# Sums of weight blocks and of hidden values for seven block products, made on VectorE in place of GpSimd

## Chip, cores and metric

The kernel runs on one core of one Trainium2 chip. The metric is the device time of one execution in microseconds (us). The engines are named as in the profile: PE (TensorE matmuls), PEld (its weight loads), DVE (VectorE), ACT (ScalarE), POOL (GpSimd) and SP (SyncE, which here issues the DMAs). Each engine runs its instructions in the order in which they stand; between engines semaphores do the waiting.

## The reference, cut to what matters

A decoder trunk of 4 layers works on 256 tokens of width 1024, in float32. Every layer has a feed-forward network (FFN), a token mixer (window attention, gated linear attention, RWKV-7, window attention again) and a second FFN, so there are eight FFNs.

```python
def swiglu(x, w_in, w_out):
    gate, up = jnp.split(x @ w_in, 2, axis=-1)
    return (jax.nn.silu(gate) * up) @ w_out

for layer in range(DEPTH):                        # DEPTH = 4, D_FF = 2816
    ff = swiglu(rmsnorm(h, g[0]), ffn_w_in[layer, 0], ffn_w_out[layer, 0])
    h = h + 0.5 * rmsnorm(ff, g[1])
    ...                                           # the layer's mixer
    ff = swiglu(rmsnorm(h, g[4]), ffn_w_in[layer, 1], ffn_w_out[layer, 1])
    h = h + 0.5 * rmsnorm(ff, g[5])
```

## The kernel before

Matmuls run in a one-pass format that holds fewer bits than float32. So every operand is **split** into a high part, copied and rounded by ACT, and a low part, value minus high part, which DVE computes with a `tensor_tensor` subtract. Each product is then three matmuls (`mm3`): high by high, high by low, low by high. Every weight block that comes from memory therefore costs one DMA, one ACT instruction and one DVE instruction over 128x512 values before PE can use it (`weight`).

An FFN's 2816 middle columns are cut into 11 chunks of 256. Chunks 0 and 1 are computed tokens first (`tokens`): one PSUM bank per token tile and chunk, 24 matmuls of 512 columns. Chunks 2 to 10 are a loop with two halves of 128 middle columns each. In a half PE makes 48 matmuls of 256 columns (gate and up for both token tiles) into one PSUM bank `p`. Then DVE reads the gate out of it (`sg`, in the profile `hf<-ps,m` of 128x256), ACT copies the up part out (`hf<-ps`), ACT takes a tanh, and two DVE instructions make the hidden values (`hf<-hf,hf`, `m<-hf,hf`). Only after the copy is `p` free for the next half.

The second matrix product of a chunk is a 2x2 by 2x2 block product (tokens in two halves, middle columns in two halves, output columns in two halves). It is made from **seven** block products in place of eight, which needs sums of blocks on both sides. On the side of the weights `weights(c)` loads four 128x512 blocks of `w_out` and makes four differences T1 to T4 from them; T2 needs T1 and T4 needs T2. On the side of the hidden values `hidden(th)` makes four 128x128 sums s1 to s4 into one tile `S`; s2 needs s1 and s4 needs s2. All of them are then split by ACT and DVE, and `products` runs 3 matmuls of 512 columns for each of the seven. The seven results stay in seven PSUM banks `acc` over all chunks. There are eight banks, so in the loop one is left for `p`. In the loop, 12 of these matmuls stand after a chunk's first half and 9 after its second; in the last chunks 6 of the 9 are put off to the end of the FFN.

The order within each engine is not the order of the code. All calls are recorded, and `schedule` sets them by a plan with costs for every instruction and a latency between engines: on each engine, the call that can start first comes next. In that plan a `tensor_tensor` of n columns costs 120 + 1.1 n ns on POOL and 70 + 1.04 n ns on DVE. Splits of weights and the weight differences may be taken ahead of their time (`kind = "split"`). Buffers of 128x512 values (tag `m`, 87 of them) are given out by the same plan, and SP, which issues all loads in order, waits for a buffer to come free. All instructions are issued from one line of `emit`, L471; L469 issues the few matmuls that keep the clock up.

The names that matter: `GT` (line 760) is the engine call that makes T1 to T4 in `weights` (line 779) and s1 to s4 in `hidden` (line 796).

Of the kernel before, what the change touches and what calls it, by code (L numbers as in the profile page):

```python
# [480 lines left out]
class Trunk:  # L481
# [264 lines left out]
    def ffn(self, l, f, start):  # L746
# [8 lines left out]
        nc = self.nc  # L755
# [1 line left out]
        w_out = self.a["ffn_w_out"][l, f].rearrange("(k p) n -> p k n", p=P)  # L757
        n0 = 6 * l + 4 * f
        uh, ul = ([self.m2([P, 2, NT, P], F32R) for _ in range(4)] for _ in "hl")
        GT = nc.gpsimd.tensor_tensor  # L760

        def load_in(c, k):
            return self.once(("ffn", l, f, c, k), lambda: self.weight(
# [8 lines left out]
        def split(x, dt):  # L772

            hi, lo = dt(), dt()
            nc.scalar.activation(hi[:], x, AF.Copy)
            nc.vector.tensor_tensor(lo[:], x, hi[:], ALU.subtract)
            return hi, lo

        def weights(c):
# [9 lines left out]
            for n, x, y in ((1, b[1, 2], b[1, 1]), (2, b[2, 2], T[1]), (4, b[2, 1], T[2]), (3, b[2, 2], b[1, 2])):  # L789
                GT(T[n][:], x[:], y[:], ALU.subtract)  # L790
            r = {n: split(w[:], lambda: self.m2(dt=F32R)) for n, w in (
# [4 lines left out]
        def hidden(th):  # L796
# [3 lines left out]
            s = [None] + [S[:, n, :] for n in range(4)]  # L800
            GT(s[1], a21, a22, ALU.add)
            GT(s[2], s[1], a11, ALU.subtract)
            GT(s[3], a11, a21, ALU.subtract)
            GT(s[4], a12, s[2], ALU.subtract)
            three = th[:].rearrange("p j t n -> p (j t) n")[:, :3]
# [932 lines left out]
```

## Time and profile before

| | |
|---|---|
| median of 3 runs | 2399.59 us (2398.52 to 2401.42) |
| the profiled execution | 2397.45 us, span from first to last instruction 2395.5 us |
| busy over the span | PE 2109.6, DVE 2029.5, ACT 1368.8, POOL 899.8 us |
| instructions | PE 14120, DVE 3292, ACT 3000, POOL 889 |
| mean granted clock of TensorE | 0.958 of full speed |
| read from memory | 351.64 MB |

A row that groups instructions says which engine, operation and tiles (output, arrow, inputs), the shape (partitions x columns), how many, how long they were busy together, the mean duration of one in ns, and the engine's idle time just before them with what ended it. DVE starts an instruction before the one ahead has fully ended, so durations add up to more than busy time. The granted clock is 1.00 at 2.4 GHz and 0.50 at 1.2 GHz; a stretch between has parts of both.

### The profile page before, as it was taken

What the parts mean: (1) busy time and instruction counts of PE and PEld (TensorE: products, weight loads), DVE (VectorE), ACT (ScalarE), POOL (GpSimd) and SP (SyncE); (2) the same over time, 40 slices, a digit from 0 to 9 for tenths busy, and PEclk for the clock granted to TensorE, in tenths of its full rate; (3) what the DMA queues carried; (4) which work ended last, traced back from release to release, by engine and by line L of the source; (5) the groups of instructions that cost most, each with busy time, mean ns of one, the idle gap of its engine ahead of it and who ended that gap; (6) DMA issues with size and microseconds to landing.
All of it is one profiled execution on the core that took longest, in us unless ns stands there. A gap on an engine that the chain in (4) does not pass through costs nothing. (4 is left out here: it accounts for less than half of the span.)

```text
span 2395.5 us, 41720 instructions
## 1 busy us (share of the span) xinstructions
PE 2109.6 (88%) x14120; PEld 1818.6 (76%) x14120; DVE 2029.5 (85%) x3292; ACT 1368.8 (57%) x3000; POOL 899.8 (38%) x889
## 2 busy tenths in 40 slices
PE   7888998888888998988888889998888888898887
PEld 6787768786777776877678768887877678777776
DVE  8887989888987988888888798588888987888887
ACT  6554666555654865555554566565555655566553
POOL 4443035435543005442644222135442544205442
PEclk8999999999999999999999999999999999999998
DMA  7555345554564454555455421454555455444551
GB/s 229 155 163 178 123 148 157 159 154 139 163 175 148 123 171 136 161 162 160 134 171 151 140 89 54 126 171 128 162 160 160 136 167 170 139 148 148 161 161 57
DMA packets 444902, 355.47 MB, mean 148 GB/s; under 512 B 33372, under 2 KB 364304, under 8 KB 444688
## 3 DMA queue, kind: packets, MB, share of 16 engines
q1 hardware_dynamic: 444688, 352.82, 48.9%
q8 instruction: 110, 1.80, 0.3%
q14 instruction: 104, 0.85, 0.1%
HBM read 351.64 MB, written 1.05 MB: 147 GB/s over the span
## 5 line engine op out<-in xcount | busy, mean ns | idle before, releaser
L471 PE MATMUL ps<-m,m 128*128 128x256 f32 (+4 forms) x12248 | 1976.2, 326 | 217.4 <-ACT hf L471 139.1
L471 PEld LDWEIGHTS ps<-m,m 128*128 128x128 f32 (+2 forms) x12248 | 1665.7, 193 | 457.8 <-ACT hf L471 177.6
L471 DVE TENSOR_TENSOR m<-m,m 128x512 fp32r<-128x512 f32 (+1 forms) x1814 | 1385.1, 816 | 148.3 <-ACT m L471 144.8
L471 ACT ACTIVATE m<-m 128x512 fp32r<-128x512 f32 (+4 forms) x1838 | 1003.8, 610 | 437.0 <-POOL m L471 335.2
L471 POOL TENSOR_TENSOR m<-m,m 128x512 f32<-128x512 f32 (+1 forms) x528 | 656.9, 1258 | 351.3 <-DMA m<-in_ffn_w_out_dram 194.6
L471 POOL TENSOR_TENSOR m<-m 128x128 f32<-128x128 f32 x176 | 131.1, 764 | 534.2 <-DVE m L471 321.1
L471 ACT ACTIVATE hf<-ps 128x256 f32<-128x256 f32 (+1 forms) x166 | 62.3, 377 | 266.4 <-DVE hf L471 244.4
L471 POOL TENSOR_TENSOR ti<-ti,nhalf 128x1 f32<-128x1 f32 (+2 forms) x60 | 50.9, 849 | 379.6 <-DVE ti L471 371.3
L471 ACT ACTIVATE m<-ps 128x512 f32<-128x512 f32 (+4 forms) x219 | 109.5, 525 | 134.2 <-PE ps L471 132.6
L471 DVE SCALAR_TENSOR_TENSOR hf<-hf,hf 128x256 f32<-128x256 f32 x144 | 99.6, 692 | 60.1 <-ACT hf L471 60.0
L471 DVE TENSOR_TENSOR m<-hf,hf 128x256 f32<-128x256 f32 x144 | 115.5, 802 | 5.0
L471 POOL TENSOR_SCALAR_AFFINE_SELECT m<-m 128x512 f32<-128x512 f32 (+1 forms) x54 | 38.6, 733 | 182.7 <-ACT m L471 182.3
L471 DVE TENSOR_TENSOR m<-m,ps 128x512 f32<-128x512 f32 (+1 forms) x112 | 60.4, 568 | 25.3 <-PE ps L471 23.3
L471 ACT ACTIVATE hf<-hf 128x256 f32<-128x256 f32 x144 | 58.9, 409 | 40.0 <-DVE hf L471 40.0
L471 DVE TENSOR_TENSOR hf<-ps,m 128x256 f32<-128x256 f32 x144 | 59.7, 415 | 21.7 <-PE ps L471 17.2
L471 PE MATMUL ps<-ident,m 128*128 128x128 f32 (+1 forms) x344 | 58.8, 281 | 4.7 <-DVE m L471 3.7
L471 ACT ACTIVATE m<-ps,gT 128x128 fp32r<-128x128 f32 (+1 forms) x192 | 53.6, 377 | 15.4 <-PE ps L471 9.1
L471 PEld LDWEIGHTS ps<-ident,m 128*128 128x128 f32 (+1 forms) x344 | 41.4, 144 | 18.5 <-DVE m L471 6.4
L471 PE MATMUL ps<-ident,hf 128*128 128x128 f32 x68 | 15.2, 308 | 45.4 <-DVE hf L471 45.4
L471 DVE SCALAR_TENSOR_TENSOR m<-ps,gT,m 128x128 fp32r<-128x128 f32 x176 | 48.5, 341 | 3.8 <-ACT m L471 3.4
L471 PEld LDWEIGHTS ps<-ident,hf 128*128 128x128 f32 x68 | 7.9, 148 | 55.1 <-DVE hf L471 38.9
L471 ACT ACTIVATE junk<-h 128x512 bf16<-128x512 f32 x48 | 30.2, 629 | 29.2 <-DVE h L471 26.7
(101 smaller groups left out, 764.1 us busy)
## 6 DMA issues: line engine op xcount, KB each, us to landing
m<-in_ffn_w_in_dram SPq DMA_DIRECT2D x1152, 128.0 KB, 2.9
m<-in_ffn_w_out_dram SPq DMA_DIRECT2D x352, 256.0 KB, 3.6
m<-in_ffn_w_in_dram SPq DMA_DIRECT2D x128, 256.0 KB, 3.8
m<-in_swa_w_qkv_dram SPq DMA_DIRECT2D x48, 256.0 KB, 2.9
m<-in_rwkv_w_rkv_dram SPq DMA_DIRECT2D x48, 256.0 KB, 3.4
m<-in_gla_w_in_dram SPq DMA_DIRECT2D x40, 256.0 KB, 3.2
m<-in_swa_w_o_dram SPq DMA_DIRECT2D x32, 256.0 KB, 2.7
m<-in_norm_g_dram SPq DMA_DIRECT2D x24, 256.0 KB, 4.8
```

What stands on the lines that cost most here:

```text
L471: getattr(getattr(self.nc, o.eng), fn)(*[fix(v) for v in args], **{k: fix(v) for k, v in kw.items()})
```

## The change

`GT` becomes the same call of DVE. The 88 chunks have eight such calls each, 704 in all. The function computes what it computed before; nothing else in the code differs.

```diff
@@ -757,7 +757,7 @@
         uh, ul = ([self.m2([P, 2, NT, P], F32R) for _ in range(4)] for _ in "hl")
-        GT = nc.gpsimd.tensor_tensor
+        GT = nc.vector.tensor_tensor
```

Because the plan's costs and the engine are others, the scheduler sets a new order for the whole program. Here is DVE's row in the third FFN, in the loop, from one reading of `p` by DVE (`hf<-ps,m`) on. The names are numbered by tile, so the same role has another number in the two programs. Before, the row is the reading, splits, and the next reading:

```order
L471 TENSOR_TENSOR hf_140_8121<-ps_156_8024,m_1423_6828 128x256
L471 TENSOR_TENSOR m_1707_8125<-m_1664_7904,m_1679_7985 128x512
L471 SCALAR_TENSOR_TENSOR hf_142_8130<-hf_142_8130,hf_140_8121 128x256
L471 TENSOR_TENSOR m_1708_8137<-hf_141_8127,hf_142_8130 128x256
L471 TENSOR_TENSOR m_1718_8159<-m_1662_7900,m_1680_7992 128x512
L471 TENSOR_TENSOR m_1721_8170<-m_1677_7975,m_1681_7995 128x512
L471 TENSOR_TENSOR m_1722_8177<-m_1668_7916,m_1682_8001 128x512
L471 TENSOR_TENSOR m_1723_8184<-m_1674_7959,m_1683_8004 128x512
L471 TENSOR_TENSOR m_1724_8191<-m_1675_7963,m_1685_8019 128x512
L471 TENSOR_TENSOR m_1725_8198<-m_1676_7971,m_1686_8021 128x512
L471 TENSOR_TENSOR hf_143_8247<-ps_157_8168,m_1423_6828 128x256
```

Now T1 (`m_1747`, from blocks `m_1705` and `m_1704`) stands just ahead of the reading, T3 (`m_1750`) in the row after T2 (`m_1749`) right behind it, and T4 (`m_1760`) after the second product of the hidden values; splits follow:

```order
L471 TENSOR_TENSOR m_1747_8349<-m_1705_8140,m_1704_8138 128x512
L471 TENSOR_TENSOR hf_146_8355<-ps_158_8259,m_1459_7015 128x256
L471 TENSOR_TENSOR m_1749_8361<-m_1703_8136,m_1747_8349 128x512
L471 TENSOR_TENSOR m_1750_8369<-m_1703_8136,m_1705_8140 128x512
L471 SCALAR_TENSOR_TENSOR hf_148_8367<-hf_148_8367,hf_146_8355 128x256
L471 TENSOR_TENSOR m_1753_8381<-hf_147_8364,hf_148_8367 128x256
L471 TENSOR_TENSOR m_1760_8397<-m_1702_8134,m_1749_8361 128x512
L471 TENSOR_TENSOR m_1762_8407<-m_1704_8138,m_1707_8146 128x512
L471 TENSOR_TENSOR m_1765_8420<-m_1702_8134,m_1709_8155 128x512
L471 TENSOR_TENSOR m_1768_8432<-m_1703_8136,m_1715_8178 128x512
```

So three of the four differences stand between a reading of `p` and the next, and one ahead of it.

POOL's row at the same place before holds a chunk's four differences and four sums and nothing else:

```order
L471 TENSOR_TENSOR m_1713_8147<-m_1712_8145,m_1711_8143 128x512
L471 TENSOR_TENSOR m_1714_8149<-m_1710_8141,m_1712_8145 128x512
L471 TENSOR_TENSOR m_1716_8153<-m_1710_8141,m_1713_8147 128x512
L471 TENSOR_TENSOR m_1729_8224<-m_1709_8139,m_1716_8153 128x512
L471 TENSOR_TENSOR m_1741_8281<-m_1708_8137 128x128 x2
L471 TENSOR_TENSOR m_1741_8281<-m_1741_8281,m_1708_8137 128x128
L471 TENSOR_TENSOR m_1741_8281<-m_1708_8137,m_1741_8281 128x128
```

The sums stand now in DVE's row, in the chunk's second half, between the second product of the hidden values (`m_1701`) and the splits of the sums (`m_1734`):

```order
L471 TENSOR_TENSOR hf_144_8245<-ps_157_8150,m_1459_7015 128x256
L471 TENSOR_TENSOR m_1728_8248<-m_1661_7923,m_1671_7969 128x512
L471 SCALAR_TENSOR_TENSOR hf_145_8251<-hf_145_8251,hf_144_8245 128x256
L471 TENSOR_TENSOR m_1701_8132<-hf_143_8241,hf_145_8251 128x256
L471 TENSOR_TENSOR m_1729_8264<-m_1701_8132 128x128 x2
L471 TENSOR_TENSOR m_1729_8264<-m_1729_8264,m_1701_8132 128x128
L471 TENSOR_TENSOR m_1731_8275<-m_1701_8132,m_1730_8266 128x384
L471 TENSOR_TENSOR m_1729_8264<-m_1701_8132,m_1729_8264 128x128
L471 TENSOR_TENSOR m_1732_8283<-m_1667_7953,m_1673_7978 128x512
L471 TENSOR_TENSOR m_1734_8294<-m_1729_8264,m_1733_8287 128x512
```

POOL's row keeps no instruction of the FFNs but the inverse roots of the norms.

## Rows read from the trace of the kernel before

**Rows 1.** The page's first part: busy time, share, instructions of each engine.

```profile
PE 2109.6 (88%) x14120; PEld 1818.6 (76%) x14120; DVE 2029.5 (85%) x3292; ACT 1368.8 (57%) x3000; POOL 899.8 (38%) x889
```

**Rows 2.** Stretches: length, busy time by engine, granted clock, DMA share and rate; eight loops.

```profile
55.00:228.60 173.60, 151.14 (x1039) 139.43 (x1038) 147.49 (x204) 94.07 (x187) 71.25 (x65) 0.96 0.55 163
...
1175.60:1355.00 179.40, 154.93 (x1039) 143.36 (x1038) 150.40 (x208) 95.69 (x191) 76.64 (x80) 0.93 0.52 155
...
sum 1404.30, PE 1218.83 PEld 1122.94 DVE 1195.42 ACT 760.09 POOL 593.46; mean PE 152.35 PEld 140.37 DVE 149.43 ACT 95.01 POOL 74.18
```

**Rows 3.** The same view of a stretch ahead of a loop and of two between FFNs.

```profile
337.00:363.90 26.90, 20.76 (x82) 15.99 (x82) 25.13 (x33) 16.65 (x38) 23.27 (x19) 0.87 0.45 136
...
245.00:330.00 85.00, 84.71 (x487) 64.95 (x487) 75.35 (x182) 54.37 (x167) 5.49 (x8) 1.00 0.46 142
800.00:900.00 100.00, 99.17 (x655) 80.07 (x655) 91.44 (x185) 75.64 (x157) 4.97 (x6) 1.00 0.53 162
```

**Rows 4.** PE in order of time: start, length of a run, count, idle time before it.

```profile
645.25 8.03 PE L471 MATMUL ps<-m,m 128*128 128x256 f32 x57 [0.74 <-ACT hf L471]
654.87 8.71 PE L471 MATMUL ps<-m,m 128*128 128x256 f32 x60 [1.59 <-ACT hf L471]
```

**Rows 5.** DVE in order of time, one chunk of the third FFN's loop.

```profile
640.74 3.70 DVE L471 TENSOR_TENSOR m<-m,m 128x512 fp32r<-128x512 f32 x6 [1.55 <-ACT m L471]
...
645.54 1.28 DVE L471 SCALAR_TENSOR_TENSOR hf<-hf,hf 128x256 f32<-128x256 f32 x1 [0.16 <-ACT hf L471]
646.85 1.41 DVE L471 TENSOR_TENSOR m<-hf,hf 128x256 f32<-128x256 f32 x1
648.18 5.88 DVE L471 TENSOR_TENSOR m<-m,m 128x512 fp32r<-128x512 f32 x6
653.99 0.41 DVE L471 TENSOR_TENSOR hf<-ps,m 128x256 f32<-128x256 f32 x1
654.32 0.68 DVE L471 TENSOR_TENSOR m<-m,m 128x512 fp32r<-128x512 f32 x1
655.16 0.43 DVE L471 SCALAR_TENSOR_TENSOR hf<-hf,hf 128x256 f32<-128x256 f32 x1 [0.15 <-ACT hf L471]
655.62 0.42 DVE L471 TENSOR_TENSOR m<-hf,hf 128x256 f32<-128x256 f32 x1
655.96 2.29 DVE L471 TENSOR_TENSOR m<-m,m 128x512 fp32r<-128x512 f32 x3
```

**Rows 6.** POOL in order of time, the same chunk.

```profile
645.01 6.09 POOL L471 TENSOR_TENSOR m<-m,m 128x512 f32<-128x512 f32 x4 [4.97 <-DMA m<-in_ffn_w_out_dram]
656.17 1.52 POOL L471 TENSOR_TENSOR m<-m 128x128 f32<-128x128 f32 x2 [5.07 <-ACT m L471]
657.66 1.44 POOL L471 TENSOR_TENSOR m<-m,m 128x128 f32<-128x128 f32 x2
```

**Rows 7.** Groups of DVE, whole span: count, busy us, mean ns, idle before.

```profile
L471 DVE TENSOR_TENSOR m<-m,m 128x512 fp32r<-128x512 f32 x1620 | 1264.9, 834 | 137.5 <-ACT m L471 136.5
L471 DVE TENSOR_TENSOR m<-hf,hf 128x256 f32<-128x256 f32 x144 | 115.5, 802 | 5.0
L471 DVE SCALAR_TENSOR_TENSOR hf<-hf,hf 128x256 f32<-128x256 f32 x144 | 99.6, 692 | 60.1 <-ACT hf L471 60.0
```

**Rows 8.** The same view of DVE, 245 to 330 us alone.

```profile
L471 DVE TENSOR_TENSOR m<-m,m 128x512 fp32r<-128x512 f32 x48 | 30.2, 684 | 0.0
```

**Rows 9.** Groups of POOL, whole span.

```profile
L471 POOL TENSOR_TENSOR m<-m,m 128x512 f32<-128x512 f32 x352 | 539.4, 1553 | 344.6 <-DMA m<-in_ffn_w_out_dram 194.6 <-DVE m L471 50.7 <-ACT m L471 38.3
L471 POOL TENSOR_TENSOR m<-m 128x128 f32<-128x128 f32 x176 | 131.1, 764 | 534.2 <-DVE m L471 321.1 <-ACT m L471 181.1 <-PE ps L471 31.9
L471 POOL TENSOR_TENSOR m<-m,m 128x128 f32<-128x128 f32 x176 | 117.8, 669 | 6.7
```

**Rows 10.** Loads of `w_out`, 600 to 720 us: from issue to landing.

```profile
DMA to landing us min/median/max: 2.4/3.0/4.4
```

**Rows 11.** DVE in order of time, chunk 0 of the second FFN.

```profile
344.94 5.74 DVE L471 TENSOR_TENSOR m<-m,m 128x512 fp32r<-128x512 f32 x4
```

## The prediction, on record before the changed kernel ran

> **What bounds the kernel now.** I read the page's first two parts first: over the span PE is busy 2109.6 us and DVE 2029.5 us of 2395.5, POOL 899.8 [rows 1]. Two engines near 85% over a program of many stages say little, so I cut the span into stretches. The kernel has eight FFNs, and in each of them chunks 2 to 10 run as a loop of about 175 us; the eight loops together take 1404.3 us, of which PE is busy 1218.8, so PE stands still for 185.5 us in them by the sum in [rows 2]. A stretch between two FFNs looks different: in 800 to 900 us POOL is busy 5.0 of 100 us, DVE 91.4, and PE 99.2 at full granted clock; in 245 to 330 us it is 5.5, 75.4 and 84.7 of 85 [rows 3]. So PE is not stopped by a DVE that is busy 91%; it is stopped where POOL works.
>
> The loop shows how. PE alternates between a run of 8.03 us (48 matmuls of the hidden values, then 9 products) followed by a wait of 1.59, and a run of 8.71 us (48 and 12) followed by 0.74 [rows 4]. The waits end with ACT's copy out of the one PSUM bank that the seven accumulators leave free; that copy stands behind DVE's read of the same bank (`hf<-ps,m`, called the evacuation below), because DVE is in order and reads it first. A chunk is thus 16.74 us of PE work and about 2.33 us of waiting.
>
> Why is the evacuation late? In the run that begins at 645.25 PE has finished the 48 matmuls at about 651.2 (653.28 less 9 products; the run of 60 is 0.68 longer than that of 57, so 0.227 each). DVE reaches the evacuation at 653.99 [rows 5], since six splits before it took 5.88 us. Six of the same splits took 3.70 at 640.74 [rows 5]: 0.684 for one, and (3.70 - 0.684)/5 = 0.603 from one start to the next. The difference, 2.18 us, falls where POOL makes the chunk's four differences of weight blocks, 645.01 to 651.10 [rows 6]. The two DVE instructions just before are stretched as well, 1.28 and 1.41 us against 0.43 and 0.42 half a chunk later, where POOL rests [rows 5]. So each 128x512 operation of POOL stops DVE for about 1.0 us, (0.85 + 0.99 + 2.18)/4. Over the program the three largest DVE groups with two SBUF inputs have means of 834, 802 and 692 ns [rows 7], where the first takes 684 in the stretch without POOL work [rows 8] and the others 0.42 and 0.43: 1620 x 0.150 + 144 x 0.38 + 144 x 0.26 = 335 us of DVE time that is only waiting for POOL.
>
> The other half of the chunk loses in a chain: POOL's four 128x128 sums take 656.17 to 659.10, ACT splits them only then, and DVE idles 1.55 us for ACT (one row shown, of the chunk before) [rows 5, 6].
>
> **What the change removes.** All 704 operations of this kind leave POOL: 352 of 128x512 at 1553 ns and 352 of 128x128 at 764 and 669 ns [rows 9]. With them go the stretch on DVE, about 4.0 us per chunk from the weights and 0.5 from the sums (655.96: three instructions in 2.29 us, about 1.75 alone [rows 5]), and the idle 1.55 us. Nothing else hides behind POOL; what remains there are square roots and masks.
>
> **What it adds.** DVE gets the same 704. A 128x512 one goes at the 0.603 us pace, so 2.4 us per chunk for four. No 128x128 operation of this form runs on DVE before. Its pace is bounded by the 256-column evacuation (0.33 from 653.99... to the next start at 654.32 [rows 5]) and, by the slope (0.603 - 0.33)/256 per column, 0.19; two of the four need the result just made, so I take 0.25 each, 1.0 us per chunk. DVE's chunk before, without the stretch: 16 instructions of 512 columns x 0.603 = 9.65, one of 384 (0.47 by the same slope), and two evacuations with their two followers 2 x (0.33 + 0.46 + 0.34) = 2.26; together 12.4 us. After: 12.4 + 3.4 = **15.8 us per chunk, under PE's 16.74** (94%). Before, with 4.5 us of stretch and the idle times, DVE came to about 19, and that was the period: it was DVE's row that PE waited for.
>
> **What moves.** The scheduler orders anew by its costs. In DVE's row the first difference of a chunk now stands just ahead of an evacuation, the second to fourth right behind it, and the four sums behind the second product of the hidden values. In the order the four buffers for a chunk's `w_out` were last read by matmuls about a hundred rows, some 14 us of PE work, ahead of the first difference, and such a load lands 2.4 to 4.4 us after its issue [rows 10]; so DVE should not have to wait for it. I cost that at nothing; if it fails, every evacuation behind it waits too (the third rival). In the order 120 clock-keeping matmuls stand where 115 stood: nothing.
>
> **The sum**, against the profiled execution (span 2395.5, time 2397.45):
> 1. Idle PE in the eight loops is 185.5. The nearest rows without POOL work leave PE idle under 1% [rows 3], 1.5 us per loop; since DVE's margin is 6% and two late halves of each FFN carry more DVE rows than PE can cover, I leave 3 us per loop, 24. Gain 161. Ends: 13 us per loop left (81) and 1 left (177).
> 2. PE's busy time in the loops is itself longer than its work. Work is 9 x 16.74 less 18 products that the last three chunks put off (4.1), 146.6 per loop, 1172.8 in all, against 1218.8: 46 us, and the granted clock there is 0.93 to 0.96, 1.00 in the busy stretches [rows 2, 3]. PE at half clock follows its waits; I give back 60%, 27 us. Ends 0 and 46.
> 3. Chunks 0 and 1, eight stretches like 337 to 363.9: DVE is busy 25.13 of 26.9, PE 20.76 [rows 3]. Eight differences and eight sums move in: 8 x 0.603 + 8 x 0.25 = 6.8 us; out goes the stretch, 8 x 1.0 and a little. Four splits there take 5.74 instead of 2.49 [rows 11], 1.08 for each of three POOL operations, so about 8.8 goes. Net gain 2 us, 16 in all. Ends 0 and 5 each.
> Sum 161 + 27 + 16 = 204: span 2191, time 2193, and 2 more to the median of the runs (2399.59): **2195 us**.
>
> **The rivals.** *DVE stays the bound, at a smaller time.* The durations of its instructions, not their paces, might count: where every one stood alone, 17 x 0.684 less a fraction, plus 2 x 1.26, plus 4 x 0.684 and 4 x 0.28 give 17.9 per chunk, over PE's 16.74. Then a loop takes 9 x 17.9 = 161 and a little, the gain is 8 x 13.5 = 108, no more in the stretches before: 2290. For it: 94% leaves little for an in-order row that waits for ACT after each difference. Against: six splits in 3.70 us, and PE at 99% beside DVE at 91% [rows 5, 3].
>
> The Trainium skill, VectorE: DVE Perf Modes, section The DRAIN you can't avoid, says that after an operation the pipe is flushed and the next does not start until it is empty (and that one which is not held starts earlier). By its first half the time would be this rival's; the trace's pace of 0.603 beside 0.684 speaks for its second.
>
> *DVE's long instructions are not POOL's doing* (slower). If they stretch for another reason, such as loads into SBUF, all 704 come on top: 9 x 3.4 = 31 us on DVE's 150 busy in a loop, 181 with nothing idle, against 175.5, and 6.8 in each stretch before: 8 x (5.5 + 6.8) = 98, 2498 us. It decides if less than about a seventh of the 335 us goes. Against it: the stretch sits exactly where POOL runs [rows 5, 6], and not in 245 to 330 [rows 8], where the DMA moves nearly as much (142 against 157 GB/s [rows 2, 3]).
>
> *The wait for `w_out` moves to DVE.* POOL waited 194.6 us for it [rows 9]. If DVE took all of that over, with evacuations behind it, 2195 + 195 = 2390: no change. Against: the order, as above.
>
> **How the numbers follow.** Forecast 0.72; DVE-bound by durations or by waits in its row 0.20; wait for `w_out` 0.04; stretch not from POOL 0.04. The range reaches down to the sum's good ends, 177 + 46 + 40 = 263, 2136, and a little for what DVE gives back elsewhere: 2130; up to the first rival, 2290. A measurement of this kernel can tell about 0.2% from no change. Faster by more than that 0.94, within 0.02, slower 0.04.
>
> **What would show it.** DVE's splits near 684 ns on average everywhere; PE's waits between runs gone or under 0.4 us, loops near 152 us; POOL busy about 110 us; granted clock above 0.97 in the loops. I am wrong if the splits stay above 750 ns (no lock), if DVE shows waits for `w_out`, or if the evacuations still start 2 us after the last of the 48 matmuls though nothing stretches, which is the in-order row itself.

## The result, and the profile after

The changed kernel takes **2117.45 us** (median of 4 runs, 2116.84 to 2119.18) against 2399.06 us before (4 runs): ratio 0.883, 95% interval 0.881 to 0.884. The forecast was 2195 us, with a range of 2130 to 2290: the direction was right, but the gain is 282 us where 204 were forecast, and the time lies 13 us below the range.

The page of the changed kernel, busy time by engine and the granted clock in 40 slices of the span (2116.1 us):

```profile
PE 2028.1 (96%) x14130; PEld 1773.2 (84%) x14130; DVE 1937.7 (92%) x3996; ACT 1364.8 (64%) x3000; POOL 118.3 (6%) x185
...
PEclk9999999999999999999999899999999999999999
```

Against [rows 1] DVE runs 704 instructions more and is busy 92 us less. POOL keeps 118 us. PE is busy 81 us less for the same matmuls (10 more to keep the clock up).

The groups of DVE (count, busy us, mean ns of one, idle before):

```profile
L471 DVE TENSOR_TENSOR m<-m,m 128x512 fp32r<-128x512 f32 x1620 | 1021.9, 687 | 23.0 <-ACT m L471 16.5
L471 DVE TENSOR_TENSOR m<-m,m 128x512 f32<-128x512 f32 x430 | 284.6, 686 | 1.6 <-ACT m L471 1.0
L471 DVE TENSOR_TENSOR m<-hf,hf 128x256 f32<-128x256 f32 x144 | 61.2, 425 | 4.9
...
L471 DVE SCALAR_TENSOR_TENSOR hf<-hf,hf 128x256 f32<-128x256 f32 x144 | 60.5, 420 | 24.5 <-ACT hf L471 24.2
L471 DVE TENSOR_TENSOR m<-m,m 128x128 f32<-128x128 f32 x176 | 50.4, 287 | 0.0
...
L471 DVE TENSOR_TENSOR m<-m 128x128 f32<-128x128 f32 x176 | 43.8, 290 | 2.5
```

The three groups of [rows 7] went from 834, 802 and 692 ns to 687, 425 and 420: the stretch is gone in all three. The 352 weight differences are in the second row, 686 ns each where POOL took 1553 [rows 9]; the sums of hidden values take 287 and 290 ns.

Half a chunk of the third FFN's loop in order of time, DVE from one evacuation to the next, and after it PE over two and a half chunks (start, length, count; a row that groups instructions bears the shape of its first, so the ten below are one difference and nine splits, and the 292 hold products of 512 columns too):

```profile
535.68 0.42 DVE L471 TENSOR_TENSOR hf<-ps,m 128x256 f32<-128x256 f32 x1
536.03 1.28 DVE L471 TENSOR_TENSOR m<-m,m 128x512 f32<-128x512 f32 x2
537.23 0.41 DVE L471 SCALAR_TENSOR_TENSOR hf<-hf,hf 128x256 f32<-128x256 f32 x1
537.68 0.42 DVE L471 TENSOR_TENSOR m<-hf,hf 128x256 f32<-128x256 f32 x1
538.02 6.10 DVE L471 TENSOR_TENSOR m<-m,m 128x512 f32<-128x512 f32 x10
544.04 0.42 DVE L471 TENSOR_TENSOR hf<-ps,m 128x256 f32<-128x256 f32 x1
```

```profile
519.78 40.59 PE L471 MATMUL ps<-m,m 128*128 128x256 f32 x292
```

Ten DVE instructions of 512 columns take 6.10 us, (6.10 - 0.684)/9 = 0.602 apart, as six did in 3.70 [rows 5]. DVE's rows show no wait here, and PE runs 40.6 us without one where it had waited 1.59 and 0.74 in turn [rows 4].

The stretches again: the sum over the eight loops of the changed kernel, over what lies outside its loops, and, third, over what lies outside them before (length; busy time of PE, PEld, DVE, ACT, POOL):

```profile
sum 1207.70, PE 1170.71 PEld 1091.32 DVE 1156.29 ACT 762.60 POOL 0.00; mean PE 146.34 PEld 136.41 DVE 144.54 ACT 95.33 POOL 0.00
```

```profile
sum 908.40, PE 857.40 PEld 681.86 DVE 781.42 ACT 602.24 POOL 118.34; mean PE 95.27 PEld 75.76 DVE 86.83 ACT 66.92 POOL 13.15
```

```profile
sum 991.20, PE 890.75 PEld 695.64 DVE 834.05 ACT 608.68 POOL 306.37; mean PE 98.97 PEld 77.29 DVE 92.67 ACT 67.63 POOL 34.04
```

With [rows 2] the 279.4 us of span divide into: loops 1404.3 to 1207.7 (197, of it 149 idle PE and 48 busy PE), outside 991.2 to 908.4 (83, of it 49 idle PE and 33 busy PE). PE does the same work in both kernels, and up to 73 of its 81 us less of busy time can be clock (an estimate): the mean granted clock rose from 0.958 to 0.987, which is some 200 us at half clock before and 55 after.

### The profile page after: what moved, and what is told of

It reads as the page before. It is cut to its first block, busy times and chain, and to the rows that moved or that the text cites. A ratio compares the mean times of both kernels' runs of the same rounds, so it can differ in the third digit from the quotient of the medians.

```text
span 2116.1 us, 41020 instructions
## 1 busy us (share of the span) xinstructions
PE 2028.1 (96%) x14130; PEld 1773.2 (84%) x14130; DVE 1937.7 (92%) x3996; ACT 1364.8 (64%) x3000; POOL 118.3 (6%) x185
## 4 chain that ended last, share of the span: by engine, by line
PE 68%; DVE 20%; DMA 4%; ACT 3%; issue 3%; POOL 1%; SPq 0%; DVEq 0%; POOLq 0%; ACTq 0%
PE ps L471 68%; DVE m L471 17%; DMA m<-in_ffn_w_in_dram 2%; ACT m L471 2%; DVE hf L471 1%; DMA m<-in_ffn_w_out_dram 1%; POOL ti L471 1%; ACT hf L471 1%; DVE ti L471 1%; DVE h L471 1%; SPq L471 0%; DMA m<-in_swa_w_qkv_dram 0%; ACT junk L471 0%; DMA m<-in_rwkv_w_rkv_dram 0%; PE ps L469 0%
## 5 line engine op out<-in xcount | busy, mean ns | idle before, releaser
L471 PE MATMUL ps<-m,m 128*128 128x256 f32 (+4 forms) x12248 | 1896.7, 319 | 56.4 <-DVE m L471 23.3
L471 PEld LDWEIGHTS ps<-m,m 128*128 128x128 f32 (+2 forms) x12248 | 1616.3, 186 | 265.3 <-DVE m L471 44.2
L471 DVE TENSOR_TENSOR m<-m,m 128x512 fp32r<-128x512 f32 (+3 forms) x2342 | 1377.3, 648 | 25.9 <-ACT m L471 18.6
L471 DVE SCALAR_TENSOR_TENSOR hf<-hf,hf 128x256 f32<-128x256 f32 x144 | 60.5, 420 | 24.5 <-ACT hf L471 24.2
L471 DVE TENSOR_TENSOR m<-hf,hf 128x256 f32<-128x256 f32 x144 | 61.2, 425 | 4.9
L471 DVE TENSOR_TENSOR m<-m 128x128 f32<-128x128 f32 (+2 forms) x201 | 56.9, 323 | 4.9 <-ACT m L471 2.4
L471 ACT ACTIVATE junk<-m 128x512 bf16<-128x512 f32 x40 | 24.9, 624 | 28.8 <-DVE m L471 28.8
L471 DVE SCALAR_TENSOR_TENSOR h<-m,ti,h 128x512 f32<-128x512 f32 x48 | 34.5, 746 | 6.0 <-POOL ti L471 5.8
L471 DVE TENSOR_TENSOR m<-ps,m 128x512 f32<-128x512 f32 (+1 forms) x44 | 29.7, 684 | 8.1 <-ACT m L471 4.4
```

Of the source, the lines that this page charges most:

```text
L471: getattr(getattr(self.nc, o.eng), fn)(*[fix(v) for v in args], **{k: fix(v) for k, v in kw.items()})
```

## The experiments

My theory at this point: POOL's sums stop DVE's instructions with two SBUF inputs; the evacuation of the one free PSUM bank, in DVE's row, then comes late, and PE waits. Three rivals: the new order of all rows gave the gain; the chain through POOL's sums of hidden values did, not the stretch; the stretch has another cause.

### Engine and order apart

Both kernels change what an operation is issued to without changing what the scheduler plans.

```diff
+        def GT(*x):
+            getattr(nc, "gpsimd").tensor_tensor(*x)   # second kernel: "vector"
+            nc.ops[-1].runs = "vector"                # second kernel: "gpsimd"
...
-                getattr(getattr(self.nc, o.eng), fn)(
+                getattr(getattr(self.nc, o.runs or o.eng), fn)(
```

Old order, sums on DVE:

> The scheduler plans as in the kernel before (sums priced and placed as POOL's), but the 704 sums are issued to DVE, so the row of every other engine stands as before. Theory (POOL's sums stop DVE, and the late read of the one free PSUM bank stops PE): most of the 282 us goes without any new order, 2140 to 2230 us. Rival (the new order, with w_out loaded some 14 us of matmul work ahead, is what gave the gain): 2330 to 2420 us.

New order, sums on POOL:

> The scheduler plans as in the changed kernel (sums priced and placed as DVE's), but the 704 sums are issued to POOL. Theory: DVE's splits are stretched again (mean over 780 ns) and the time is 2350 us or more, since nothing in the plan knows that POOL needs over 1.2 us for each. Rival (the order gave the gain): under 2250 us.

Measured: 2245.15 us (ratio 0.935, 0.933 to 0.938) and 2403.27 us (1.001, 1.000 to 1.003). The new order alone is worth nothing; the engine alone 154 us, with the time 15 us above the range that I had set for it; both together 282. So the order is worth 128 us, but only with the sums on DVE. DVE's splits show why nothing is gained in the second kernel:

```profile
L471 DVE TENSOR_TENSOR m<-m,m 128x512 fp32r<-128x512 f32 x1620 | 1334.0, 879 | 101.5 <-ACT m L471 101.2
```

What the first one lacks is told by whom its PE and its DVE wait for (engine, line, waited for: us in total, times, longest):

```profile
PE ps L471 <- DVE hf L471: 74.6, 30, 5.4
PE ps L471 <- ACT hf L471: 61.4, 51, 3.4
...
DVE m L471 <- DMA m<-in_ffn_w_out_dram: 28.0, 24, 3.7
```

The same two waits of PE before, and then in the changed kernel:

```profile
PE ps L471 <- ACT hf L471: 139.1, 83, 4.2
PE ps L471 <- DVE hf L471: 91.1, 33, 6.2
```

```profile
PE ps L471 <- DVE hf L471: 18.3, 17, 1.4
...
PE ps L471 <- ACT hf L471: 4.6, 8, 1.5
```

DVE's wait for `w_out` is not among the changed kernel's waits over 3.7 us in total. The splits take 688 ns in the old order too, so nothing is stretched. But its DVE row was made without the sums: 3 us per chunk stand in places that were planned full, and PE waits for the evacuations again. DVE also waits 28 us for `w_out`, as POOL had; that is the prediction's third rival, and with the new order it is gone. How the 128 us divide between the two no run shows.

### Which sums

```diff
-        GT = nc.gpsimd.tensor_tensor
+        GT, GV = nc.gpsimd.tensor_tensor, nc.vector.tensor_tensor
...
-                GT(T[n][:], x[:], y[:], ALU.subtract)     # weights alone
+                GV(T[n][:], x[:], y[:], ALU.subtract)
...
-            GT(s[1], a21, a22, ALU.add)                   # the other kernel: s[1] to s[4] alone
+            GV(s[1], a21, a22, ALU.add)
```

> Only the four weight differences per chunk (128x512) go to DVE; the four sums of hidden values stay on POOL. Theory (the stretch counts, 4.0 of 4.5 us per chunk are the weights'): 2130 to 2200 us. Rival (what counts is the chain through POOL's sums, with ACT and DVE idle behind it): over 2260 us.

> Only the four sums of hidden values per chunk (128x128) go to DVE; the weight differences stay on POOL. Theory: the stretch by the weights stays, so 2320 to 2400 us. Rival (the chain through the sums counts): under 2260 us.

Measured: 2207.33 us (0.920, 0.918 to 0.922) and 2348.68 us (0.979, 0.976 to 0.981). The weight differences carry 192 us, with the time 7 us above the range that I expected, and the sums of hidden values 50; 242 together, 40 less than both at once. The rival that the chain through the sums of hidden values is the cause falls: most of the gain goes with the weight differences, which carry most of the stretch (DVE's splits take 708 ns in the first kernel and 845 in the second). But the scheduler plans each of these kernels anew, and with the weight differences on DVE, ACT no longer waits for POOL to make them (ACT's waits for POOL's `m` were 335 us before). That the stretch by itself is enough is shown only by the readers below.

### Which chunks

```diff
+        def engine(c):
+            return (nc.vector if c < OLD else nc.gpsimd).tensor_tensor   # the other kernel: c >= OLD
...
-            b = {}
+            b, GT = {}, engine(c)
```

> Sums of chunks 0 and 1 alone go to DVE (16 per FFN); those of the loop's chunks 2 to 10 stay on POOL. By the prediction's third term this gives 16 us, so 2383 us (ends 0 and 40: 2399 and 2359). By the traces, in which the time outside the loops fell by 83 us, about 2316 us. If the two places depend on each other (the sums of the loop reach into the stretches between), something between.

> Sums of chunks 2 to 10 alone go to DVE; those of chunks 0 and 1 stay on POOL. By the prediction's first two terms this gives 188 us, so 2211 us; by the traces, in which the loops fell by 197 us, about 2202 us. If the gain outside the loops comes from the loops' sums as well, nearer to 2150 us.

Measured: 2366.96 us (0.987, 0.985 to 0.990) and 2157.31 us (0.900, 0.898 to 0.902). The loops' sums bring 241 us, nearest to the last of the three times that I had set for them, and those of chunks 0 and 1 31, between the two times that I had set; 272 of 282. Where it shows is another matter. With the sums of chunks 0 and 1 alone the time outside the loops fell by 51.5 us, three times the 16 of the prediction, and the loops grew by 21.5, to 1425.8. With the loops' sums alone the loops fell by 220, more than in the changed kernel, and the rest by 18, to 973.4:

```profile
sum 939.70, PE 874.46 PEld 691.18 DVE 788.93 ACT 609.86 POOL 183.43; mean PE 97.16 PEld 76.80 DVE 87.66 ACT 67.76 POOL 20.38
```

```profile
sum 1184.60, PE 1161.69 PEld 1084.94 DVE 1113.14 ACT 764.48 POOL 13.68; mean PE 145.21 PEld 135.62 DVE 139.14 ACT 95.56 POOL 1.71
```

The first is the time outside the loops with chunks 0 and 1 alone on DVE, the second the eight loops with the loops' sums alone. So the border between the two places moves with the order: the scheduler takes work of the stretch ahead into the loop. Counted in the traces by their starts, the loops hold 1155 of the 512-column splits and 1385 matmuls of 512 columns before, and 1189 and 1452 after. The 67 matmuls, 15 us at 0.23 each, are loop time now.

The new order with the sums on POOL has the same border. First its time outside the loops, then its loops; third, the time outside the loops for the old order with the sums on DVE:

```profile
sum 951.00, PE 872.36 PEld 683.19 DVE 793.38 ACT 603.51 POOL 250.32; mean PE 96.93 PEld 75.91 DVE 88.15 ACT 67.06 POOL 27.81
```

```profile
sum 1450.20, PE 1274.41 PEld 1166.54 DVE 1214.76 ACT 757.82 POOL 634.00; mean PE 159.30 PEld 145.82 DVE 151.84 ACT 94.73 POOL 79.25
```

```profile
sum 964.70, PE 881.78 PEld 690.89 DVE 830.58 ACT 611.59 POOL 116.04; mean PE 97.98 PEld 76.77 DVE 92.29 ACT 67.95 POOL 12.89
```

Against the kernel before, the order alone takes 40 us off the time outside the loops and puts 46 on the loops; the engine alone takes 26.5 off outside.

### POOL's work put back, reading or writing

Into the changed kernel, behind each of the 352 weight differences, one instruction of POOL (first kernel) or five (second) whose result nobody reads; no other row changes.

```diff
                 getattr(getattr(self.nc, o.eng), fn)(*[fix(v) for v in args], **{k: fix(v) for k, v in kw.items()})
+                if o.echo:
+                    t, x = (fix(v)[:, :384] for v in args[:2])       # second kernel: [:, :1]
+                    self.nc.gpsimd.tensor_tensor(self.scratch[:], t, x, ALU.add)   # second: scratch[:, :1]
+                    for _ in range(4):                               # second kernel alone
+                        self.nc.gpsimd.memset(self.scratch[:], 0.0)
```

> The changed kernel with one more instruction on POOL behind each of the 352 weight differences: a sum of 384 columns of that difference and of one of its inputs into a tile that nobody reads; nothing else moves in any row. Theory (an instruction of POOL that reads SBUF stops a DVE instruction with two SBUF inputs for its whole length): each costs DVE some 0.75 us, 3 us per chunk over DVE's 15.8, past PE's 16.2, so 2270 to 2400 us, with the mean of the splits over 730 ns. Rival (the stretch was not POOL's doing): 2117 to 2130 us.

> The changed kernel with, behind each of the 352 weight differences, one POOL sum of a single column and four POOL memsets of 384 columns into a tile that nobody reads: POOL is about as long busy as with one sum of 384 columns, but it only writes. Theory (POOL's reads stop DVE): 2117 to 2190 us, the single columns costing at most some 0.4 us each of DVE time where they meet a split; the splits' mean under 700 ns. Rival (any work of POOL stops DVE): as with the sums of 384 columns, 2270 to 2400 us.

Measured: 2392.3 us (0.998 of the kernel before, 0.996 to 0.999) and 2133.96 us (0.890, 0.888 to 0.893). The readers alone undo the whole change: 275 us for 352 instructions whose results no engine waits for. The writers cost 16.5 us. That a buffer comes free later because POOL still reads it is not the reason: SP's waits for a buffer that POOL ends come to 18.3 us with the readers and to 100.5 with the writers. POOL's groups in the two kernels, the reader's first, then the writer's:

```profile
L474 POOL TENSOR_TENSOR scratch<-m,m 128x384 f32<-128x384 f32 x352 | 441.6, 1255 | 1131.8 <-DVE m L471 688.8 <-DMA m<-in_ffn_w_in_dram 330.9 <-issue 48.6
```

```profile
L476 POOL MEMSET scratch<- 128x384 f32 x1408 | 593.5, 422 | 81.7
```

and DVE's two largest groups, again reader first:

```profile
L471 DVE TENSOR_TENSOR m<-m,m 128x512 fp32r<-128x512 f32 x1620 | 1122.0, 746 | 25.1 <-ACT m L471 22.2
L471 DVE TENSOR_TENSOR m<-m,m 128x512 f32<-128x512 f32 x430 | 344.4, 824 | 1.5 <-ACT m L471 1.0
```

```profile
L471 DVE TENSOR_TENSOR m<-m,m 128x512 fp32r<-128x512 f32 x1620 | 1022.2, 686 | 30.0 <-ACT m L471 23.5 <-POOL scratch L474 3.4
L471 DVE TENSOR_TENSOR m<-m,m 128x512 f32<-128x512 f32 x430 | 284.0, 684 | 4.3 <-POOL scratch L474 2.9 <-ACT m L471 0.8
```

POOL is busier in the second kernel (863.5 us) than in the first (561.6), and there DVE runs at 686 ns as without it. DVE's busy time with the readers is 2178.0 against 1937.7 us, 0.68 us for each of the 352; I had set 0.75, and my theory's "for its whole length" is too much, since a reader lasts 1.26 us. PE's wait for DVE's `hf` is back with them, 154.4 us against 18.3. The rival that the stretch is not POOL's doing falls, and so does the one that any work of POOL stops DVE: it is POOL's reading of SBUF against DVE's instructions with two inputs there. The Trainium skill, SBUF — State Buffer, section Who interferes with whom, says just this (a DVE instruction with two SBUF inputs contends with a GpSimd instruction that reads SBUF, not with one that only writes it); the two traces agree, with 746 and 824 ns against 686 and 684.

DVE's evacuation has two inputs too, but one of them lies in PSUM. With the readers it takes

```profile
L471 DVE TENSOR_TENSOR hf<-ps,m 128x256 f32<-128x256 f32 x144 | 59.8, 415 | 45.3 <-PE ps L471 37.5 <-ACT hf L471 7.7
```

against 422 ns without them, and the 23 of them that in the trace lie for more than half their length beside a reader take 423 on average. Counting inputs does not tell the whole, though. A `tensor_scalar` of DVE with one input, in SBUF, was stretched as well. Its row before the change:

```profile
L471 DVE TENSOR_SCALAR m<-m 128x512 f32<-128x512 f32 x28 | 22.5, 828 | 10.8 <-DMA m<-in_norm_g_dram 10.8
```

The same group takes 419 ns after the change and 490 with the writers. So this form is held up by POOL's writing too, where the two-input ones are not. It weighs little here, with 28 instructions.

### What bounds the changed kernel

The rows in the changed kernel's order, with a POOL memset of the same tile in place of each sum.

```diff
+                if o.zero:
+                    self.nc.gpsimd.memset(fix(args[0]), 0.0)
+                    continue
```

> The changed kernel with every row in its order, but the 704 sums are left out of DVE: a POOL memset of the same tile, which only writes, stands in for each (the sums are zero, so this is the time of a kernel without them). It takes 3.2 us per chunk, 283 us in all, from DVE. Theory (PE is the bound now, idle 88 us of 2116): 2060 to 2112 us. Rival (DVE, busy 92%, is still the bound): below 2000 us.

Measured: 2071.2 us (0.863, 0.861 to 0.866). DVE is 270 us less busy and the time falls by 46:

```profile
PE 2015.6 (97%) x14130; PEld 1770.2 (85%) x14130; DVE 1667.2 (80%) x3292; ACT 1354.9 (65%) x3000; POOL 348.9 (17%) x889
```

PE is the bound of the changed kernel. What all the sums together still cost on DVE is some 46 us, or a little more if the 704 memsets on POOL cost time themselves.

## Why the prediction was wrong in size, step by step

- **What bounds the kernel, and why.** Right. The stretch of DVE by POOL is shown by the runs that take it away or put it back. PE's waits for the `hf` of DVE and ACT go and return with it: 230 us in all before, 23 after, 161 with the readers. The late evacuation between the two was not tried by itself.
- **DVE's cost.** Right. 0.602 us from start to start where 0.603 was taken; DVE is busy 144.5 us per loop, 16.1 per chunk, where 15.8 was worked out. The first rival (durations count, not paces) falls with it.
- **Term 1, idle PE in the loops.** 149 us where 161 was forecast, with 4.6 us left per loop in place of 3. The loops take 151 us on average; the forecast said near 152. That rests on the new order as well: in the old order with the sums on DVE the eight loops take 1272.2 us, 132 less than before and not 197.
- **Term 2, PE's busy time in the loops.** 48 where 27 was forecast, 2 past its upper end, though 15 us of matmuls moved in. I gave back 60% of what half clock had cost; the granted clock in the loops is now 0.99 to 1.00 by the same view as [rows 2], so nearly all of it came back. Summed from the clock's own records, the loops had 137 us at half clock and have 10 now; PE was busy in 123 of them and is in 10, which by half the difference is worth some 56 us (an estimate). The 46 that I had as the whole was too little, because 16.74 us is too much for a chunk's work: without a wait two and a half chunks take 40.59 us, 16.2 each.
- **Term 3, the time outside the loops: the step that failed.** Forecast 16 (ends 0 and 40), measured 83. I priced it as the net of DVE's busy time in the stretch ahead of a loop, 8.8 us out and 6.8 in, and took PE's and DVE's idle times and the clock there for given, though the first two terms had treated just these as the gain. DVE's busy time outside the loops fell by 52.6 us, 6.6 per FFN and not 2: of POOL's 704 sums 176 had stood outside the loops, 22 per FFN and not the 16 that I counted, so more was stretched; now 128 sums stand there, and 34 splits went into the loops with the other 48 sums. The remaining 30 us are idle time of DVE. Seen from PE, 49 of the 83 us are idle time, and of the 33 of busy time 15 are the moved matmuls. The old order with the sums on DVE shows how far my arithmetic was good: there the time outside the loops is 964.7, a gain of 26.5. The other 56 needed the new order. "What moves" says what it moves, but the only effect priced there is DVE's wait for `w_out`, at nothing; the sum had no term for work that changes place. The order by itself takes 40 us off outside the loops, and with the sums on POOL the loops pay it back with 46. With the sums on DVE they do not.
- **The range** ended at 2130 because its lower end allowed term 3 at most 40. Half clock outside the loops (67 us before, visible in the clock of 0.87 in [rows 3], and 45 after), PE's idle time there and the moved work were not in it.
- **The slower rivals.** The stretch is POOL's. The wait for `w_out` exists in DVE's row where the order is the old one, 28 us, and not in the changed kernel, as the order had said.

What stays open: how much of the 56 us outside the loops is the work moved into them and how much the better filling of what remains. The 15 us of matmuls and the 40 us that the order takes off by itself speak for the moved work, but no run separates the two, as every change of the plan changes both. That half clock came from PE's waits was not tried by itself either; the two went away together.

## What to carry to other kernels

Before pricing work on a second engine as free, compare the durations of the first engine's same instruction in stretches with and without the second at work: here 834 against 684 ns told that 788 us of work on an "idle" engine cost some 335 us on the busy one. When one cause makes an engine wait, apply the same terms (idle time, clock) to every stretch of the program, not only to the one in which it was found. And where a scheduler sets the order, a plan that knows the new cost can be worth nearly as much as the move (128 us of 282), yet nothing without the move.

## What was not expected

- 352 reading instructions on POOL whose results nobody uses took the whole gain back (2117 to 2392 us), while 745 us of added POOL work that mostly writes cost 0.8%.
- Single sums of one column on POOL, 352 of them at 430 ns, are among that 0.8%: a short read stops DVE little.
- With the sums left out altogether, PE's idle time in the loops, the sum over them in the same view, is 1164.7 - 1159.0 = 5.7 us: the loop can run at PE's pace with the one PSUM bank that is left for `p`.

```profile
sum 1164.70, PE 1159.02 PEld 1088.29 DVE 916.32 ACT 753.78 POOL 190.58; mean PE 144.88 PEld 136.04 DVE 114.54 ACT 94.22 POOL 23.82
```
